# Two weight sums of every third block made by accumulating transfers, weight sums as additions, and a new order inside halved blocks

## The chip, the cores and the metric

The kernel runs on one core of a Trainium2 chip. The metric is device time in microseconds (us) of one execution. Engines are named as in the profile: PE multiplies matrices, DVE (VectorE) and ACT (ScalarE) work on whole tiles of 128 partitions, POOL (GpSimd) issues the transfers that accumulate, SP (SyncE) issues the loads. The kernel has three results before: the median is 1452.87 us (1452.65 to 1453.44).

## The reference

The reference is one decoder layer on a sequence of 256 tokens of width 2048, in float32: a mixing part (block-sparse attention and a gated short convolution, each through its branch weights), then an MLP, then a gated embedding of each layer. Cut to the MLP, which is where the change is:

```
h  = rms_norm(x, g_mlp)
u  = square(relu(h @ w_up))      # 256 x 8192
x  = x + u @ w_down              # 8192 -> 2048
```

The output goes on to the gated embedding and is written out as 256 x 2048.

## The kernel before, in words

**Precision.** Each float32 operand is split into a high part in a faster float32 format and the remainder: ACT copies the tile (`high`), DVE subtracts the copy from the source (`low`). A product is three matmuls, high by high, high by low and low by high. So each weight tile costs an ACT copy and a DVE subtraction ahead of its matmuls.

**The MLP's steps.** The MLP runs as 72 steps, numbered g. Each of the first 64 steps multiplies one 128-column tile of w_up by all of h (`cols`, 32 matmuls into one bank of PSUM, bank 7, called ps_up). ACT copies that bank out (`up`), DVE adds its two halves (`a<-up`), ACT does relu and square, and the result is one 128-row slice of u. The last eight steps take tiles of w_down directly in the same way (ps_dn).

**Blocks.** The rest of w_down is multiplied by the method of seven products in place of eight: a block is a 2 x 2 arrangement of weight pieces B11, B12, B21, B22 (each 128 x 512), and a 2 x 2 of pieces of u. Sums of weight pieces (T1 to T4) and sums of u pieces (S1 to S4) are formed on DVE, and seven products are accumulated in seven banks. There are 56 blocks. Block a = (side, j) is made in one step and multiplied by PE in the next, behind that step's `cols`. Per full block DVE does: `low` of B11 and B22 (`b_lo`, 128x1024), two sums in one instruction of 128x1024 (`raw_s<-raw_s`), a sum of 128x512, `low` of B21 (`b`, 128x512), a sum of 128x512, and `low` of T1/T3 and of T2/T4 (`t_lo`, two of 128x1024). A block whose u sums don't exist yet (called fresh here) adds four sums of 128x128 (`s_raw`) and their `low` (`s`, 128x512). The two tiles of w_up per step add two `w_lo` of 128x1024.

**Halved blocks.** Blocks (0,0), (0,9) and (0,24) to (0,31) are spread over two steps each: the first makes B11, B22 and T1, T3, the second B21 and T2, T4. The last sixteen steps that make blocks, 55 to 70, are all of this kind.

**Parts and jobs.** The seven banks hold one side of the output. When the run of blocks of a side ends, ACT copies the banks out (`part`) and POOL stores them to DRAM, adding to what is there (`part_P`, seven transfers). This comes six times, around steps 10, 18, 27, 35, 43 and 51; four of the stores are carried into the next step. In steps 54 to 66 the finished parts are fetched again (`raw_p`, through the ring of four large tiles that the weights use too), scaled and combined, two small jobs per step. The last job of each is `turn`: DVE transposes in blocks, POOL stores the turned tiles (turned_s), reads them back in the other order (part_in), and adds them to r_kept in DRAM. Toward the end `load_r` loads r from r_kept, and `dn_done` adds the direct results (y_dn) to it, both on POOL. ACT and DVE then make the input of the gated embedding from r (`enter_high`, `enter_low`).

**Order.** The order on PE, DVE, ACT and SP is the order in which the code is written. POOL's DMA issues stand in the order written too. `make` writes the steps of one block; the function passed to it as `evacuate` is the copy `up` (or `dn`) of the step's bank, and PE's next step can start only when that copy is done. `fill` emits a pending part store if there is one. `half_tiles` takes weight tiles from two rings of eight, tags hi and lo; for half of the blocks, T2/T4 used a spare ring of two, tag t.

Of the kernel before, what the change touches and what calls it, by code (L numbers as in the profile page):

```python
# [8 lines left out]
F32 = mybir.dt.float32  # L9
# [29 lines left out]
def hybrid_block_kernel(ctx: ExitStack, tc: tile.TileContext, ins: dict, out: bass.AP):  # L39
# [632 lines left out]
    def half_tiles(name, spare=False):  # L672
        return tuple(wp.tile([P, HALF], F32R, tag="t" if spare else t, name=f"{name}_{t}", bufs=2 if spare else None) for t in ("hi", "lo"))
# [9 lines left out]

    def load_pair(a):

        side, j = a
        q, k, n0 = j // 8, 2 * (j % 8), 8 * side
        raw = wp.tile([P, 4, CW], F32, tag="raw", name="raw_s", bufs=4)
        for i, (n, d) in enumerate(((0, 0), (4, 1), (4, 0), (0, 1))):
            n += 16 * q + n0  # L690
            src = ins["w_down"][n:n + 4, :, (k + d) * P:(k + d + 1) * P]
            load(raw[:, i, :].rearrange("p (n m) -> p n m", n=4), src.rearrange("n p m -> p n m"))
        wS[a] = {"raw": raw}

    def sum_u(j):
# [21 lines left out]
    def make(a, xs, evacuate):  # L717
# [4 lines left out]
        flat = "p a f -> p (a f)"  # L722
        fresh = None
        if 0 in xs:
# [22 lines left out]
        if 0 in xs:  # L747
            dve.tensor_sub(raw[:, 0:3:2, :], raw[:, 0:2, :], raw[:, 2:3, :].to_broadcast([P, 2, CW]))
        if 2 in xs:
            dve.tensor_add(raw[:, 1, :], raw[:, 1, :], raw[:, 0, :])  # L750
            low(b21[1], raw[:, 3, :], b21[0])
            dve.tensor_sub(raw[:, 3, :], raw[:, 1, :], raw[:, 3, :])
        if fresh is not None:
            low(sl, fresh, sh)
        halves = "p (a f) -> p a f"
        if 0 in xs:
            t13 = w["t13"] = half_tiles("t13")
            keep(w, ("T1", "T3"), *t13)
            view = [t.rearrange(halves, a=2) for t in t13]
            high(view[0], raw[:, 0:3:2, :])  # L760
            fill()
            low(view[1], raw[:, 0:3:2, :], view[0])
        if 2 in xs:
            t24 = half_tiles("t24", items.index(a) % 2 == 0)
            keep(w, ("T2", "T4"), *t24)
            view = [t.rearrange(halves, a=2) for t in t24]
            high(view[0], raw[:, 1:4:2, :])
            fill()
            low(view[1], raw[:, 1:4:2, :], view[0])
# [151 lines left out]
    for g in range(NU):  # L921
# [277 lines left out]
```

## Time and profile before

| what | value |
|---|---|
| median of three runs | 1452.87 us |
| profiled execution, its own time | 1451.77 us |
| its span | 1450.0 us |
| busy: PE, DVE, ACT, POOL | 98%, 79%, 61%, 15% |
| steps 8 to 53 of the MLP | 681.69 to 1166.45 us |
| steps 54 to 66 | 1166.45 to 1298.51 us |
| steps 67 to 70 | 1298.51 to 1330.63 us |

Times of the trace are us from the start of the span. The profiled execution took 1.77 us more than its span. A row of a timeline gives the start, the length, the engine, the line of the code (that of the helper which emits it), the operation with the tile written and the tiles read, the shape, how many instructions the row holds, and in brackets how long the engine stood idle before it and what ended that. PE's rows are pipelined: a matmul is longer than the distance to the next.

### The profile page before, as it was taken

How to read it: one execution, taken by the hardware profiler on the slowest of the kernel's cores; microseconds unless marked ns; L12 is line 12 of the kernel's file. 1: busy time of each engine (PE TensorE's matmuls, PEld its weight loads, DVE VectorE, ACT ScalarE, POOL GpSimd, SP SyncE). 2: the span in 40 equal slices, each digit the busy share in tenths (PEclk: the TensorE clock that was granted, in tenths of full speed). 3: DMA queues.
4: the chain of work that ended last, by engine and by line, in shares of the span. 5: the costliest groups of instructions: out<-in, count | busy, mean ns of one | idle time of the engine just before them, and what ended most of it. 6: DMA issues, size and time to landing. Idle time of an engine off the chain costs nothing.

```text
span 1450.0 us, 19774 instructions
## 1 busy us (share of the span) xinstructions
PE 1420.0 (98%) x7009; PEld 1194.6 (82%) x7009; DVE 1144.8 (79%) x1722; ACT 884.8 (61%) x1438; POOL 220.4 (15%) x343
## 2 busy tenths in 40 slices
PE   9999999999999999999999999999999998889998
PEld 7888888888888888888887888888788887778888
DVE  7676566666565657757999999999999998888984
ACT  6765545554544445446777777777777776656652
POOL 0033564402020200000100101001010102242000
PEclk9999999999999999999999999999999999989999
DMA  9867787766665665644765867769686767999370
GB/s 289 295 223 251 230 249 229 234 208 202 209 225 202 215 254 199 222 157 153 221 233 188 264 200 202 244 196 247 202 232 207 206 215 239 279 282 270 135 265 23
DMA packets 208371, 318.81 MB, mean 220 GB/s; under 512 B 13840, under 2 KB 134928, under 8 KB 194192
## 3 DMA queue, kind: packets, MB, share of 16 engines
q1 hardware_dynamic: 190272, 280.79, 59.1%
q0 software_dynamic: 17856, 36.72, 10.3%
q8 instruction: 55, 0.90, 0.2%
q14 instruction: 44, 0.36, 0.1%
q10 hardware_dynamic: 144, 0.04, 0.0%
HBM read 290.23 MB, written 26.74 MB: 219 GB/s over the span
## 4 chain that ended last, share of the span: by engine, by line
PE 58%; DVE 26%; issue 7%; ACT 6%; DMA 2%; POOL 0%; SPq 0%; DVEq 0%; ACTq 0%; POOLq 0%
PE ps_g L90 12%; PE ps_o L90 7%; PE ps_pg L90 6%; PE ps_y L90 6%; DVE w_lo L101 6%; DVE raw_s L101 5%; DVE b_lo L101 4%; DVE t_lo L101 4%; PE ps_up L90 3%; PE ps_q L90 3%; PE ps_k L90 3%; PE ps_cx L90 3%; PE ps_cb L90 3%; PE ps_cc L90 3%; PE ps_v L90 3%
## 5 line engine op out<-in xcount | busy, mean ns | idle before, releaser
L101 DVE TENSOR_TENSOR w_lo<-raw,w_hi 128x512 fp32r<-128x512 f32 (+1 forms) x524 | 467.9, 926 | 186.6 <-ACT w_hi L87 161.5
L87 ACT ACTIVATE w_hi<-raw 128x512 fp32r<-128x512 f32 (+1 forms) x524 | 407.3, 816 | 262.4 <-PE ps_g L90 63.1
L90 PE MATMUL ps_up<-x,w_hi 128*128 128x512 f32 x1024 | 260.1, 397 | 15.1 <-ACT up L87 15.1
L90 PEld LDWEIGHTS ps_up<-x,w_hi 128*128 128x128 f32 x1024 | 192.3, 190 | 63.5 <-ACT up L87 26.4
L87 ACT ACTIVATE t_hi<-raw_s 128x1024 fp32r<-128x1024 f32 x112 | 119.0, 1062 | 126.8 <-DVE raw_s L101 125.4
L90 PE MATMUL ps_g<-w_hi,x 128*128 128x512 f32 x512 | 158.2, 389 | 0.0
L101 DVE TENSOR_TENSOR raw_s<-raw_s 128x1024 f32<-128x1024 f32 x168 | 146.0, 869 | 5.4
L101 DVE TENSOR_TENSOR t_lo<-raw_s,t_hi 128x1024 fp32r<-128x1024 f32 x112 | 134.7, 1220 | 16.7 <-ACT t_hi L87 16.7
L90 PEld LDWEIGHTS ps_up<-x,w_lo 128*128 128x128 f32 x1024 | 131.3, 191 | 5.0
L90 PE MATMUL ps_up<-x,w_lo 128*128 128x256 f32 x1024 | 132.8, 283 | 0.0
L90 PE MATMUL P<-t_hi,s 128*128 128x512 f32 x336 | 121.7, 389 | 0.0
L90 PEld LDWEIGHTS ps_g<-w_hi,x 128*128 128x128 f32 x512 | 96.1, 188 | 20.0
L800 POOL DMA_DIRECT2D part_P<-part x42 | 31.9, 777 | 485.9 <-ACT part L87 404.4
L90 PE MATMUL ps_g<-w_lo,x 128*128 128x512 f32 x256 | 99.6, 389 | 0.0
L90 PE MATMUL ps_y<-w_hi,x 128*128 128x512 f32 x256 | 79.4, 389 | 0.0
L90 PEld LDWEIGHTS P<-t_hi,s 128*128 128x128 f32 x336 | 63.1, 188 | 12.7
L101 DVE TENSOR_TENSOR b_lo<-raw_s,b_hi 128x1024 fp32r<-128x1024 f32 x56 | 68.2, 1218 | 3.6 <-ACT b_hi L87 3.6
L90 PE MATMUL ps_pg<-x,w_hi 128*128 128x512 f32 (+1 forms) x272 | 68.4, 381 | 1.3 <-DVE x L101 1.3
L90 PE MATMUL P<-t_lo,s 128*128 128x512 f32 x168 | 65.4, 389 | 0.0
L87 ACT ACTIVATE a<-a 128x256 f32<-128x256 f32 x128 | 53.2, 415 | 16.9 <-DVE a L101 15.0
L87 ACT ACTIVATE b_hi<-raw_s 128x1024 fp32r<-128x1024 f32 x56 | 58.8, 1050 | 3.2 <-DMA raw_s<-in_w_down_dram 3.2
L90 PEld LDWEIGHTS ps_pg<-x,w_hi 128*128 128x128 f32 x272 | 49.2, 189 | 10.1 <-DVE x L101 2.6
(234 smaller groups left out, 2488.9 us busy)
## 6 DMA issues: line engine op xcount, KB each, us to landing
raw<-in_w_up_dram SPq DMA_DIRECT2D x64, 1024.0 KB, 7.6
raw<-in_w_in_dram SPq DMA_DIRECT2D x56, 1024.0 KB, 5.3
raw_s<-in_w_down_dram SPq DMA_DIRECT2D x224, 256.0 KB, 4.3
raw<-in_w_branch_dram SPq DMA_DIRECT2D x16, 1024.0 KB, 5.7
raw<-in_w_o_dram SPq DMA_DIRECT2D x16, 1024.0 KB, 5.0
raw_first<-in_w_qkv_dram SPq DMA_DIRECT2D x48, 256.0 KB, 6.8
raw<-in_w_qkv_dram SPq DMA_DIRECT2D x12, 1024.0 KB, 6.2
part_P<-part POOLq DMA_DIRECT2D x42, 256.0 KB, 7.3
```

The lines of the kernel that those rows point to most:

```text
L87: return inorder(nc.scalar.activation(*args, **kw))
L90: return inorder(nc.tensor.matmul(*args, **kw))
L101: return lambda *args, **kw: inorder(getattr(nc.vector, name)(*args, **kw))
L800: nc.gpsimd.dma_start(parts[side, name], st, **how)
```

## The change

1. Every third block from the fifth to the forty-seventh (15 blocks) is "added". Its first two weight sums, B11 + B12 and B22 + B12 in the new signs, are no longer made by DVE. SP loads B12 twice into a tile `t13` of the spare ring, two steps ahead, and POOL issues two transfers with `accum_op=add` that bring B11 and B22 onto it. The piece B12 isn't loaded into `raw` for these blocks.
2. All weight sums are additions; the signs move into the u sums and the scalings (`scaled` gets a parameter for subtraction).
3. The copy `up` (`evacuate`) stands right behind the copy of B11 and B22, ahead of the copy of the u sums.
4. T2/T4 always come from the rings hi and lo.
5. In halved blocks DVE has other work between a sum and the `low` that needs ACT's copy of it: the second half makes both sums first, then `low` of B21, then the jobs; the first half runs the jobs between `low` of the u sums and `low` of T1/T3. Since the jobs are now run from inside `make` in these places, a step with a full block runs none.

```diff
-    def half_tiles(name, spare=False):
-        return tuple(wp.tile([P, HALF], F32R, tag="t" if spare else t, name=f"{name}_{t}", bufs=2 if spare else None) for t in ("hi", "lo"))
+    def half_tiles(name):
+        return tuple(wp.tile([P, HALF], F32R, tag=t, name=f"{name}_{t}") for t in ("hi", "lo"))
...
+    ADDED = set(items[4:2 * N_BOTH:3])
...
+    BLOCKS = ((0, 0), (4, 1), (4, 0), (0, 1))
     def load_pair(a):
...
+        for i, block in enumerate(BLOCKS):
+            if i != 2 or a not in ADDED:
+                load(raw[:, i, :].rearrange("p (n m) -> p n m", n=4), pair_part(a, *block))
+
+    def load_added(a):
+
+        wS[a] = {}
+        if a in ADDED:
+            t = wS[a]["t13"] = wp.tile([P, 2, CW], F32, tag="t", name="t13", bufs=2)
+            view = [t[:, i, :].rearrange("p (n m) -> p n m", n=4) for i in range(2)]
+            for i in range(2):
+                load(view[i], pair_part(a, *BLOCKS[2]))
+            for i in range(2):
+                nc.gpsimd.dma_start(view[i], pair_part(a, *BLOCKS[i]), accum_op=ALU.add)
...
             high(hi, src)
-            fill()
+            evacuate()
             if fresh is not None:
                 high(sh, fresh)
-            fill()
             low(lo, src, hi)
-            evacuate()
+            if a in ADDED:
+                t13 = w["t13"]
+            else:
+                t13 = raw[:, 0:3:2, :]
+                dve.tensor_add(t13, raw[:, 0:2, :], raw[:, 2:3, :].to_broadcast([P, 2, CW]))
+            w["raw13"] = t13
         if 2 in xs:
...
-            if 0 not in xs:
-                evacuate()
+            evacuate()
             fill()
+            dve.tensor_add(raw[:, 1, :], raw[:, 1, :], w["raw13"][:, 0, :])
+            if 0 in xs:
+                low(b21[1], raw[:, 3, :], b21[0])
+                dve.tensor_add(raw[:, 3, :], raw[:, 1, :], raw[:, 3, :])
+                raw24 = raw[:, 1:4:2, :]
+            else:
+                dve.tensor_add(raw[:, 2, :], raw[:, 1, :], raw[:, 3, :])
+                low(b21[1], raw[:, 3, :], b21[0])
+                raw24 = raw[:, 1:3, :]
+                work()
         if 0 in xs:
...
+            if fresh is not None:
+                low(sl, fresh, sh)
+            if 2 not in xs:
+                work()
...
+        for a, x in staged[g + 2]:
+            if x == 0:
+                load_added(a)
...
+        def run_jobs():
+            for _ in range(min(2, len(jobs))):
+                jobs.pop(0)()
+
         fill(carried)
         if staged[g]:
-            make(staged[g][0][0], [x for _, x in staged[g]], take)
+            make(staged[g][0][0], [x for _, x in staged[g]], take, run_jobs)
         take()
-        for _ in range(min(2, len(jobs))):
-            jobs.pop(0)()
```

On DVE, the work of one added block that is not fresh (made in step 10), first before the change, then after it. `t_6098` is the tile t13 that the transfers fill; `raw_s` is the block's loaded tile.

```order
L101 TENSOR_TENSOR x<-a,x 128x256
L101 TENSOR_TENSOR b_lo<-raw_s,b_hi 128x1024
L101 TENSOR_TENSOR raw_s<-raw_s 128x2x512
L101 TENSOR_TENSOR raw_s<-raw_s 128x512
L101 TENSOR_TENSOR b_1_6386<-raw_s,b_0_6385 128x512
L101 TENSOR_TENSOR raw_s<-raw_s 128x512
L101 TENSOR_TENSOR t_lo<-raw_s,t_hi 128x1024 x2
L101 TENSOR_TENSOR a<-up 128x256
```

```order
L101 TENSOR_TENSOR x<-a,x 128x256
L101 TENSOR_TENSOR b_lo<-raw_s,b_hi 128x1024
L101 TENSOR_TENSOR raw_s<-raw_s,t_6098 128x512
L101 TENSOR_TENSOR b_1_6390<-raw_s,b_0_6389 128x512
L101 TENSOR_TENSOR raw_s<-raw_s 128x512
L101 TENSOR_TENSOR t_lo<-t_6098,t_hi 128x1024
L101 TENSOR_TENSOR t_lo<-raw_s,t_hi 128x1024
L101 TENSOR_TENSOR a<-up 128x256
```

The 128x2x512 sum (shown as 128x1024 in the profile) is gone, and the first 128x512 sum and the first `t_lo` read the tile t13.

On DVE, the second half of block (0,24) (step 56), first before, then after. `raw_p` are the fetched parts; `blocks` are their transposes.

```order
L101 TENSOR_TENSOR raw_s<-raw_s 128x512
L101 TENSOR_TENSOR b_1_11136<-raw_s,b_0_11135 128x512
L101 TENSOR_TENSOR raw_s<-raw_s 128x512
L101 TENSOR_TENSOR t_lo<-raw_s,t_hi 128x1024
L101 SCALAR_TENSOR_TENSOR raw_p<-raw_p,scales 128x256 x2
L101 STREAM_TRANSPOSE blocks<-raw_p 128x512 x2
L101 TENSOR_TENSOR a<-up 128x256
```

```order
L101 TENSOR_TENSOR raw_s<-raw_s 128x512 x2
L101 TENSOR_TENSOR b_1_11177<-raw_s,b_0_11176 128x512
L101 SCALAR_TENSOR_TENSOR raw_p<-raw_p,scales 128x256 x4
L101 TENSOR_TENSOR t_lo<-raw_s,t_hi 128x1024
L101 TENSOR_TENSOR a<-up 128x256
```

The jobs moved ahead of `t_lo`, and they are other jobs: the transposes that stood in step 56 stand in step 57 after the change, as each later pair of jobs stands one step later.

## Rows read from the trace of the kernel before

**Rows 1.** The page's busy line, and DVE's busy share in 40 equal slices of the span, in tenths.

```profile
PE 1420.0 (98%) x7009; PEld 1194.6 (82%) x7009; DVE 1144.8 (79%) x1722; ACT 884.8 (61%) x1438; POOL 220.4 (15%) x343
...
DVE  7676566666565657757999999999999998888984
```

**Rows 2.** Busy time by stretch: length, then PE, PEld, DVE, ACT and POOL busy (instructions), PE's granted clock, the DMA engines' share and GB/s. Steps 8 to 53, 54 to 66 and 67 to 70.

```profile
681.69:1166.45 484.76, 476.89 (x2419) 402.01 (x2418) 466.66 (x610) 357.26 (x520) 31.89 (x42) 1.00 0.73 219
1166.45:1298.51 132.06, 117.93 (x576) 98.33 (x575) 119.42 (x178) 80.63 (x118) 34.61 (x52) 0.94 0.81 247
1298.51:1330.63 32.12, 32.09 (x172) 27.49 (x171) 28.62 (x41) 18.05 (x22) 11.42 (x16) 1.00 1.01 287
```

**Rows 3.** The same view for steps 14 to 21, one by one: a dense step, a step with fresh sums, the step of the part stores, and the sum of the eight.

```profile
745.20:755.53 10.33, 10.33 (x55) 8.86 (x53) 10.19 (x16) 7.58 (x11) 0.00 (x0) 1.00 0.69 220
...
766.29:777.48 11.19, 10.64 (x53) 8.78 (x54) 11.05 (x17) 7.87 (x12) 0.00 (x0) 1.00 0.60 197
...
799.00:809.76 10.76, 10.49 (x54) 8.68 (x52) 8.82 (x11) 9.23 (x16) 3.78 (x7) 1.00 0.95 295
...
sum 85.35, PE 83.81 PEld 70.59 DVE 82.52 ACT 62.67 POOL 3.78; mean PE 10.48 PEld 8.82 DVE 10.31 ACT 7.83 POOL 0.47
```

**Rows 4.** Waits from 681 to 1166 us: who waited for whom, in total, times, and the longest, in us.

```profile
ACT t_hi L87 <- DVE raw_s L101: 92.8, 90, 2.0
PE ps_up L90 <- ACT up L87: 7.9, 21, 0.6
```

**Rows 5.** ACT's timeline in step 49, a fresh one.

```profile
1122.28 0.63 ACT L87 ACTIVATE s<-s_raw 128x512 fp32r<-128x512 f32 x1 [1.26 <-DVE s_raw L101]
1122.82 0.58 ACT L87 ACTIVATE up<-ps_up 128x512 f32<-128x512 f32 x1
```

**Rows 6.** PE's timeline at the start of step 50.

```profile
1123.45 0.96 PE L90 MATMUL ps_up<-x,w_hi 128*128 128x512 f32 x3 [0.55 <-ACT up L87]
```

**Rows 7.** Groups of DVE instructions of one shape from 640 to 1400 us: busy us, mean ns of one, idle time before them.

```profile
L101 DVE TENSOR_TENSOR raw_s<-raw_s 128x1024 f32<-128x1024 f32 x56 | 68.6, 1225 | 1.9
```

**Rows 8.** DVE's timeline in steps 54 to 66.

```profile
1181.76 1.00 DVE L101 SCALAR_TENSOR_TENSOR raw_p<-raw_p,scales 128x256 f32<-128x256 f32 x2
1182.68 0.42 DVE L101 TENSOR_TENSOR a<-up 128x256 f32<-128x256 f32 x1
...
1207.33 1.23 DVE L101 TENSOR_TENSOR raw_s<-raw_s 128x1024 f32<-128x1024 f32 x1
1208.47 0.68 DVE L101 TENSOR_TENSOR s<-s_raw,s 128x512 fp32r<-128x512 f32 x1
1209.67 1.22 DVE L101 TENSOR_TENSOR t_lo<-raw_s,t_hi 128x1024 fp32r<-128x1024 f32 x1 [0.52 <-ACT t_hi L87]
...
1218.19 1.23 DVE L101 TENSOR_TENSOR t_lo<-raw_s,t_hi 128x1024 fp32r<-128x1024 f32 x1 [1.13 <-ACT t_hi L87]
...
1293.23 2.31 DVE L101 TENSOR_TENSOR w_lo<-raw,w_hi 128x1024 fp32r<-128x1024 f32 x2
...
1299.46 1.23 DVE L101 TENSOR_TENSOR t_lo<-raw_s,t_hi 128x1024 fp32r<-128x1024 f32 x1 [1.19 <-ACT t_hi L87]
1300.60 2.35 DVE L101 TENSOR_TENSOR w_lo<-raw,w_hi 128x1024 fp32r<-128x1024 f32 x2
```

**Rows 9.** ACT's timeline, two waits for loads in steps 63 and 65.

```profile
1258.08 2.01 ACT L87 ACTIVATE w_hi<-raw 128x1024 fp32r<-128x1024 f32 x2 [1.92 <-DMA raw<-in_w_down_dram]
...
1284.42 1.06 ACT L87 ACTIVATE b_hi<-raw_s 128x1024 fp32r<-128x1024 f32 x1 [2.06 <-DMA raw_s<-in_w_down_dram]
```

**Rows 10.** PE's timeline, the starts of steps 58 and 66.

```profile
1207.36 1.11 PE L90 MATMUL ps_up<-x,w_hi 128*128 128x512 f32 x3 [3.30 <-ACT up L87]
...
1287.71 2.50 PE L90 MATMUL ps_dn<-x,w_hi 128*128 128x512 f32 x5 [3.82 <-ACT dn L87]
```

**Rows 11.** The chain behind the last turn: POOL's timeline (its first and its last transfer), the landing of the last one (KB each, us from issue to landing), and ACT's first read of what it brings.

```profile
1293.01 2.16 POOL L826 DMA_DIRECT2D turned_s<-blocks  x4 [6.24 <-DVE blocks L101]
...
1328.92 0.89 POOL L903 DMA_DIRECT2D r<-y_dn  x1 [0.42 <-DVE y_dn L101]
...
r<-y_dn POOLq DMA_DIRECT2D x1, 128.0 KB, 6.6
...
1338.01 0.91 ACT L87 ACTIVATE x<-r,vec 128x256 fp32r<-128x256 f32 x2
```

**Rows 12.** The DMA view of two windows of 20 us: from 976 to 996 the queue of POOL's transfers (packets, MB, share of 16 engines) and the landing of its part stores (KB each, median us), and from 1000 to 1020 the queue of SP's loads.

```profile
q0 software_dynamic: 1008, 1.84, 56.0%
...
part_P<-part POOLq DMA_DIRECT2D x6, 256.0 KB, 8.7
...
q1 hardware_dynamic: 4565, 4.53, 68.5%
```

**Rows 13.** A window with part stores, 885 to 916: its busy time as in rows 2, the landing of the raw_s loads issued from 896 to 911, and ACT's copy of the piece B21 of one of these blocks.

```profile
885.00:916.00 31.00, 30.75 (x158) 26.04 (x157) 28.85 (x34) 24.07 (x37) 6.10 (x7) 1.00 1.01 262
...
DMA to landing us min/median/max: 6.3/6.9/12.6
...
909.17 0.62 ACT L87 ACTIVATE b<-raw_s 128x512 fp32r<-128x512 f32 x1
```

**Rows 14.** DVE's and POOL's timelines at a set of part stores, step 52.

```profile
1152.14 1.23 DVE L101 TENSOR_TENSOR w_lo<-raw,w_hi 128x1024 fp32r<-128x1024 f32 x1 [0.17 <-ACT w_hi L87]
...
1152.89 1.75 POOL L800 DMA_DIRECT2D part_P<-part  x2 [0.57 <-ACT a L87]
```

More of the change, by code (lines that the diff above doesn't have):

```diff
@@ L682, in unit_half, with pair_part @@
         return lambda: high(hi, raw), lambda: low(lo, raw, hi)
+    ADDED = set(items[4:2 * N_BOTH:3])
+    def pair_part(a, n, d):
+        side, j = a
+        n += 16 * (j // 8) + 8 * side
+        k = 2 * (j % 8) + d
+        return ins["w_down"][n:n + 4, :, k * P:(k + 1) * P].rearrange("n p m -> p n m")
+    BLOCKS = ((0, 0), (4, 1), (4, 0), (0, 1))
     def load_pair(a):
-        side, j = a
-        q, k, n0 = j // 8, 2 * (j % 8), 8 * side
         raw = wp.tile([P, 4, CW], F32, tag="raw", name="raw_s", bufs=4)
[L689 to L693, printed above, removed]
+        wS[a]["raw"] = raw
+        for i, block in enumerate(BLOCKS):
[10 more added lines that the diff above has]
+                nc.gpsimd.dma_start(view[i], pair_part(a, *BLOCKS[i]), accum_op=ALU.add)
     def sum_u(j):
@@ L743, in make @@
             high(b21[0], raw[:, 3, :])
-            if 0 not in xs:
-                evacuate()
+            evacuate()
             fill()
-        if 0 in xs:
[L748 to L757, printed above, removed]
+            dve.tensor_add(raw[:, 1, :], raw[:, 1, :], w["raw13"][:, 0, :])
[8 more added lines that the diff above has]
+                work()
+        if 0 in xs:
+            if fresh is not None:
+                low(sl, fresh, sh)
+            if 2 not in xs:
+                work()
+            t13 = half_tiles("t13")
             keep(w, ("T1", "T3"), *t13)
             view = [t.rearrange(halves, a=2) for t in t13]
-            high(view[0], raw[:, 0:3:2, :])
+            high(view[0], w["raw13"])
             fill()
-            low(view[1], raw[:, 0:3:2, :], view[0])
+            low(view[1], w["raw13"], view[0])
         if 2 in xs:
-            t24 = half_tiles("t24", items.index(a) % 2 == 0)
+            t24 = half_tiles("t24")
             keep(w, ("T2", "T4"), *t24)
             view = [t.rearrange(halves, a=2) for t in t24]
-            high(view[0], raw[:, 1:4:2, :])
+            high(view[0], raw24)
             fill()
-            low(view[1], raw[:, 1:4:2, :], view[0])
+            low(view[1], raw24, view[0])
     PRODUCTS = ((("P1", "A11", "B11", 0, 3), ("P3", "S4", "B22", 0, 3)),
@@ L800, in store, with scaled @@
         nc.gpsimd.dma_start(parts[side, name], st, **how)
-    def scaled(dst, src, by, plus):
-        dve.scalar_tensor_tensor(dst, src, by, plus, op0=ALU.mult, op1=ALU.add)
+    def scaled(dst, src, by, other, how=ALU.add):
+        dve.scalar_tensor_tensor(dst, src, by, other, op0=ALU.mult, op1=how)
     ORDER = ("P5", "P4", "P2", "P3", "P1", "P7", "P6")
@@ L1058, in hybrid_block_kernel @@
     enter_low(15)
-    scaled(c12, prod["P6"], up0, e)
-    scaled(c22, prod["P5"], down1, u3)
+    scaled(c12, prod["P6"], down0, e)
+    scaled(c22, prod["P5"], up1, u3, ALU.subtract)
     half_gate(0, 1)
```

18 lines of the change are left out of this document (9 added, 9 removed).

## The prediction

> **What bounds the kernel now.** I read the page's busy shares and slices first, then busy time by stretch, then single steps, then the waits, and last the timelines of DVE, ACT and POOL where the change touches them.
>
> PE is busy 98% of the span, which looks like the end of the matter, but a PE that waits for a bank still counts as busy here. DVE stands at nine tenths or more in a row only from slice 20 to slice 33 (689 to 1196 us) [rows 1]; that is the MLP. Four stretches matter [rows 2]: steps 8 to 53 (484.76 us), steps 54 to 66 (132.06 us), steps 67 to 70, and the tail. In the first DVE is busy 466.66 us of 484.76, in the second 119.42 of 132.06, while PE's clock there falls to 0.94 because PE waits.
>
> A step in which PE is never late takes 10.33 us (the first row of [rows 3]). Eight steps, one whole round of the block pattern, take 85.35; eight times 10.33 is 82.64. So 2.71 us per eight steps is PE's wait on something else, and DVE is that: the steps of four fresh sums (11.19 us) have DVE busy 11.05, and only the step of the seven part stores (799.00) leaves it about 2 us idle [rows 3]. The waits say the same: ACT's largest is for DVE's weight sums (92.8 us), and PE waits in its turn for ACT's copy out of the bank, `up` [rows 4]. In fresh steps that copy stands behind the copy of `s`, which waits 1.26 us for DVE, and PE then starts 0.55 us late [rows 5, 6]. Over 46 steps, two of them short, the excess is 44 / 8 x 2.71, about 14.9 us. That is the most the full stretch can give.
>
> **Part by part.** *Two sums by transfers.* 15 of the 46 steps lose the 128x1024 sum. One takes 1225 ns [rows 7]; its slot, from its start to the next start, is 1208.47 - 1207.33 = 1.14 us [rows 8]. DVE saves 15 x 1.14 = 17.1 us, per eight steps 17.1 x 8 / 46 = 3.0, so it needs 85.35 - 3.0 = 82.4 where PE needs 82.64. DVE goes just below PE, PE becomes the bound, and most of the 14.9 comes back: I take 13.5, bounds 9 and 14.9. The low bound is for pockets where fresh steps with one added block among four still cost DVE more than 10.33; the earlier copy of `up` (next) is what evens these out.
>
> *`up` ahead of `s`.* In the fresh steps the bank comes free 1.26 + 0.54 = 1.8 us sooner [rows 5]. In the dense steps that is hidden already. It is no term of its own: it lets DVE's surplus in one step be repaid in the next without PE seeing it. Bounds 0 and the 0.55 us of [rows 6] in about 20 fresh steps, 11 us, which lies inside the 14.9.
>
> *Halved blocks.* Before, DVE stands 0.52 us (steps of b and s) and 1.13 us (steps of b21) ahead of `t_lo`, waiting for ACT's `t_hi` [rows 8]. After, the jobs stand in these gaps, and they are long enough (0.87 to 1.8 us). The jobs of step 54 are no longer run there, because a full block doesn't call them: the whole chain of jobs is one step later, and so is the last turn, in step 66 in place of 65. DVE starts step 55 at 1182.68 [rows 8]; after, 17.1 us plus the 1.00 of step 54's jobs earlier, near 1164.6. From there to the end of the last turn, where w_lo starts, it took 1293.23 - 1182.68 = 110.5 us. Take away the gaps, 6 x 0.52 + 5 x 1.13 = 8.8. Add what stands ahead of the turn in step 66: from 1293.23 to 1300.60 less the wait of 1.19 and the slot of t_lo, 1300.60 - 1299.46, that is 5.0, and the 1.00 of the job that left step 54. That gives 1272.3. Now the loads: raw_p's buffers come free a step later and the loads behind them land later. Before, ACT already waited 1.92 and 2.06 us for such loads [rows 9]. I add 8 us over the 12 steps, four waits of the size of [rows 9]; bounds 0 (those two as they are, which the 110.5 holds already) and 18 (one of 2 us in nine of the steps). The last turn ends near 1280.3, 12.9 earlier than in the profile.
>
> PE's own gaps here, 3.30 and 3.82 us the largest [rows 10], close by themselves when DVE is early. By PE alone the kernel would end some 25 us sooner: 13.5, these two (7.1), and about 5 of the other waits of the stretch, which are shorter.
>
> *The chain behind the last turn.* This is what turns 25 into less. After the last turn POOL stores the turned tiles, reads them back as part_in, adds them to r_kept, loads r, and adds y_dn: from 1293.2 (the end of the transposes) to 1328.92 + 6.6 = 1335.5 [rows 11], 42.3 us. Four transfers stand in it one behind the other, and each waits for the one before. ACT reads the result at 1338.01 [rows 11], so before it had 2.5 us to spare and decided nothing. After, it starts at 1280.3 and lands at 1322.6, and ACT can read no sooner: 1322.6 - 1338.0 = -15.4. PE would have been there at about -25. The chain therefore sets the end.
>
> *Transfers.* What the DVE doesn't add, the DMA engines do. An added block has one more plain 256 KB load and two accumulating ones of 256 KB in 512 B pieces. The trace has plain ones of that shape: a window with 4.53 MB of loads is 68.5% of 20 us [rows 12], so 256 KB take about 0.8 us of all 16 engines. It has accumulating ones only in longer pieces: 1008 packets, 1.84 MB, 56.0% of 20 us [rows 12], 1.6 us for 256 KB. By bytes the two new ones cost 3.2 us; by packets (178 ns each, 512 of them over 16 engines) 5.7 each, 11.4. I take 2 us each, near the byte end, because a plain transfer of 512 B pieces costs little over its share by bytes. Per three steps (31 us) that is 0.8 + 4 = 4.8, so the share rises from 0.73 [rows 2] to 0.88: still room. Where the part stores run it is 1.01 already [rows 13], raw_s lands 12.6 us after its issue there, and yet ACT's copy of it at 909.17 had no wait [rows 13]. Six such windows, each with one or two added blocks: I put a third to half a microsecond on each, 2 us in all, bounds 0 and 12.
>
> By the Trainium skill (DMA: Bandwidth & Descriptors, "Anatomy of one DMA", the GpSimd path) one such transfer takes 2.0 us plus its bytes over 436e3, that is 2.6 us for 256 KB. The trace disagrees: the part stores land 8.7 us after issue [rows 12], on engines that are busy with other queues. By the rule the 2 us would vanish and the time would be 2 lower.
>
> *POOL* gets 30 issues of 0.86 us [rows 14] where it was idle, in the queue of the part stores. An accumulate waits for its load, and stores behind it wait too; nothing reads those soon. *The signs* cost nothing: same operations, same shapes. *Tiles:* t24 now takes from the ring of 8 each time, five tiles per step in place of 4.5. A tile comes round after 1.6 steps, by when its matmuls are over; if that cover fails it is at most 1 us in a full step.
>
> Sum: -15.4 (chain) + 2 = -13.4 against the profiled run of 1451.8. That run lies 1.1 below the median of the three, 1452.9, so I predict 1452.9 - 13.4 = 1439.5.
>
> **Rivals.** *The chain doesn't bind* (0.13). With PE waiting less in the tail's loads, or fewer late loads than my 8 us, the end follows PE: -20 to -25, near 1430. For it: 42.3 us is latency under a busy DMA (1.01 in the stretch from 1298 [rows 2]), and would shrink if the loads finish early. Against: the same loads are still to be made then.
>
> *Transfers eat it* (0.20). In the windows at share 1.01 t13 isn't there in time: load 12.6 us and accumulation up to 9 or more behind each other, against two steps, 20.7, plus the part of a step until it is read. Each of some ten blocks loses 0.7 us more: -13.4 + 7 = -6, 1447. Against: rows 13 show a margin.
>
> *Slower: DMA becomes the bound* (0.07). If a 512 B accumulating packet costs 178 ns like a 2 KB one, three steps need 0.73 x 31 + 0.8 + 11.4 = 34.8 us of 31: 46 steps take 46 / 3 x 34.8 = 534 in place of 484.8, about 1490 with what is saved later. It decides from 119 ns per packet, where the share reaches 1. For it: no such packet is in the trace. Against: 512 B plain ones are cheap.
>
> *POOL's issues hold DVE* (0.02). If each of 30 issues stopped a DVE operation for its 0.86 us, 26 us would come back: -13.4 + 26 = +13, 1465. Against: the w_lo at 1152.14 took 1.23 us with POOL issuing part stores under it [rows 14], no more than any other. The Trainium skill (SBUF — State Buffer, "Who interferes with whom") says that a VectorE instruction with two SBUF inputs contends with a GpSimd instruction that reads SBUF; w_lo has two such inputs, and this row shows no stop beside DMA issues.
>
> *No change* (0.06): accumulation so late that DVE waits as long as the sum took.
>
> The forecast itself has 0.52.
>
> **How the numbers follow.** A measurement tells 0.2%, 2.9 us, from no change. Faster: 0.52 + 0.13 + 0.20 = 0.85. Same: 0.06. Slower: 0.07 + 0.02 = 0.09. The range reaches from 1430 (the chain doesn't bind) to 1449 (transfers eat most of it); the likeliest case alone spans 1435 to 1444.
>
> **What would show it.** Right: steps 14 to 21 take 82.6 to 83.5 us; 41 sums of 128x1024 instead of 56 in the MLP; no DVE wait ahead of `t_lo` in halved steps; POOL's last r<-y_dn released by r_kept and ACT's read of x<-r waiting for it; a DMA share near 0.88 in the first stretch. Wrong: DVE's first sum waiting for a DMA into t; a DMA share of 1 throughout; raw_s late in many full steps; PE never waiting at the tail.

## The result and the profile after

| | before | after |
|---|---|---|
| median, us | 1452.76 (1452.32 to 1453.44, 4 runs) | 1440.38 (1437.59 to 1441.77, 4 runs) |
| ratio to before | | 0.9912, 95% interval 0.9895 to 0.9929 |
| profiled execution, us | 1451.77 | 1440.91 |
| its span, us | 1450.0 | 1439.1 |
| steps 8 to 53 | 484.76 | 474.78 |
| steps 54 to 66 | 132.06 | 121.75 |
| steps 67 to 70 | 32.12 | 34.14 |
| from step 71 to the end | 119.37 | 126.88 |

The forecast was 1439.5. The kernel is 12.4 us faster by the medians and 10.9 by the two profiled executions. The table shows the shape of it: about 20 us are gained up to step 66 and 9.5 are given back behind it.

Busy time by stretch after the change, columns as in [rows 2]; the second stretch is steps 54 to 66:

```profile
681.55:1156.33 474.78, 471.96 (x2418) 402.87 (x2416) 449.22 (x596) 355.68 (x520) 71.44 (x72) 1.00 0.90 248
1156.33:1278.08 121.75, 112.21 (x574) 94.55 (x575) 113.51 (x169) 80.99 (x118) 29.25 (x44) 0.99 0.84 249
1278.08:1312.22 34.14, 32.17 (x171) 27.40 (x170) 30.93 (x46) 18.07 (x22) 12.43 (x18) 1.00 1.00 299
1312.22:1439.10 126.88, 114.10 (x659) 99.28 (x657) 96.32 (x167) 64.59 (x111) 6.09 (x7) 0.97 0.45 153
```

DVE has 17.4 us less to do in steps 8 to 53 and PE is busy for nearly all of them; the DMA share has gone from 0.73 to 0.90. The same view for steps 14, 16 and 19, and the sum of the eight, beside [rows 3]:

```profile
743.77:754.10 10.33, 10.33 (x55) 8.86 (x53) 10.19 (x16) 7.03 (x11) 0.00 (x0) 1.00 0.84 265
...
764.42:774.75 10.33, 10.33 (x54) 8.86 (x53) 10.21 (x16) 7.82 (x12) 0.00 (x0) 1.00 0.52 172
...
795.40:805.84 10.44, 10.44 (x55) 8.68 (x53) 8.50 (x11) 9.24 (x16) 3.62 (x7) 1.00 0.98 325
...
sum 82.87, PE 82.87 PEld 70.81 DVE 80.10 ACT 62.07 POOL 11.70; mean PE 10.36 PEld 8.85 DVE 10.01 ACT 7.76 POOL 1.46
```

The eight steps took 85.35 us and take 82.87, against 82.64 for a PE that never waits. PE's waits for `up`, 7.9 us in 21 places before [rows 4], are one of 0.8 us (the row of the same view after):

```profile
PE ps_up L90 <- ACT up L87: 0.8, 1, 0.8
```

In the halved blocks the gaps of [rows 8] are closed. DVE's waits for `t_hi` ahead of `t_lo` are 1.0 us in two places from 1156 to 1300, both behind step 66, where they were 10.0 us in 12 from 1166 to 1300. DVE's timeline in steps 55 and 56, after; these `t_lo` have no wait:

```profile
1178.06 1.00 DVE L101 SCALAR_TENSOR_TENSOR raw_p<-raw_p,scales 128x256 f32<-128x256 f32 x2
1178.98 1.22 DVE L101 TENSOR_TENSOR t_lo<-raw_s,t_hi 128x1024 fp32r<-128x1024 f32 x1
...
1184.99 1.79 DVE L101 SCALAR_TENSOR_TENSOR raw_p<-raw_p,scales 128x256 f32<-128x256 f32 x4
1186.70 1.22 DVE L101 TENSOR_TENSOR t_lo<-raw_s,t_hi 128x1024 fp32r<-128x1024 f32 x1
```

The chain behind the last turn, beside [rows 11]: POOL's first transfer of it, its last, and ACT's reads of r for n = 10 and n = 11.

```profile
1282.81 2.20 POOL L852 DMA_DIRECT2D turned_s<-blocks  x4 [0.22 <-issue]
...
1322.35 0.96 POOL L929 DMA_DIRECT2D r<-y_dn  x1
...
1322.26 0.50 ACT L87 ACTIVATE x<-r,vec 128x256 fp32r<-128x256 f32 x1
1327.70 0.51 ACT L87 ACTIVATE x<-r,vec 128x256 fp32r<-128x256 f32 x1 [4.95 <-DMA r<-y_dn]
```

Before, ACT read both at once, at 1338.01, and waited for nothing. Now the read of n = 11 waits 4.95 us for the last transfer of the chain, and all that follows waits with it. That is where the time from step 71 on goes; why steps 67 to 70 take 2.0 us more no run singles out. The steps themselves were ready sooner. ACT's copy of the last direct result, before and after:

```profile
1336.37 0.60 ACT L87 ACTIVATE dn<-ps_dn 128x512 f32<-128x512 f32 x1 [0.57 <-PE ps_dn L90]
```

```profile
1319.32 0.57 ACT L87 ACTIVATE dn<-ps_dn 128x512 f32<-128x512 f32 x1
```

That is 17.05 us earlier, and the read that waits for the chain is 10.7 us earlier.

### The profile page after: what moved, and what is told of

The parts are those of the page before. It is cut to its first block, busy times and chain, and to the rows that moved or that the text cites. A ratio compares the mean times of both kernels' runs of the same rounds, so it can differ in the third digit from the quotient of the medians.

```text
span 1439.1 us, 19915 instructions
## 1 busy us (share of the span) xinstructions
PE 1410.3 (98%) x7009; PEld 1191.7 (83%) x7009; DVE 1127.1 (78%) x1707; ACT 883.8 (61%) x1438; POOL 259.5 (18%) x373
## 4 chain that ended last, share of the span: by engine, by line
PE 69%; DVE 12%; DMA 11%; issue 4%; ACT 2%; POOL 1%; SPq 0%; DVEq 0%; POOLq 0%; ACTq 0%
PE ps_g L90 12%; PE ps_up L90 11%; PE P L90 7%; PE ps_o L90 7%; PE ps_pg L90 6%; PE ps_y L90 6%; PE ps_k L90 3%; PE ps_q L90 3%; PE ps_v L90 3%; PE ps_cx L90 3%; PE ps_cb L90 3%; PE ps_cc L90 3%; DMA part_in<-turned_s 3%; DVE w_lo L101 2%; DVE t_lo L101 2%
## 5 line engine op out<-in xcount | busy, mean ns | idle before, releaser
L90 PE MATMUL ps_up<-x,w_hi 128*128 128x512 f32 x1024 | 254.3, 391 | 6.3 <-ACT up L87 6.3
L87 ACT ACTIVATE t_hi<-raw_s 128x1024 fp32r<-128x1024 f32 x97 | 103.0, 1062 | 115.5 <-DVE raw_s L101 115.5
L101 DVE TENSOR_TENSOR raw_s<-raw_s 128x512 f32<-128x512 f32 (+1 forms) x138 | 117.3, 850 | 5.4 <-DMA raw_s<-in_w_down_dram 1.1
L101 DVE TENSOR_TENSOR t_lo<-raw_s,t_hi 128x1024 fp32r<-128x1024 f32 x97 | 116.9, 1219 | 4.4 <-ACT t_hi L87 4.4
L711 POOL DMA_DIRECT2D t<-in_w_down_dram x30 | 39.1, 1556 | 320.1 <-DVE raw_s L101 94.0
L101 DVE TENSOR_TENSOR b_lo<-raw_s,b_hi 128x1024 fp32r<-128x1024 f32 x56 | 68.3, 1220 | 3.8 <-ACT b_hi L87 3.8
```

The costliest lines, as they stand in the source:

```text
L87: return inorder(nc.scalar.activation(*args, **kw))
L90: return inorder(nc.tensor.matmul(*args, **kw))
L101: return lambda *args, **kw: inorder(getattr(nc.vector, name)(*args, **kw))
L711: nc.gpsimd.dma_start(view[i], pair_part(a, *BLOCKS[i]), accum_op=ALU.add)
```

## The experiments

The edits are to the changed kernel. Each was timed against the kernel before; the ratio and its interval stand with each median.

**No added block (e1).**

```diff
-    ADDED = set(items[4:2 * N_BOTH:3])
+    ADDED = set()
```

> The changed kernel with no added block: DVE makes all sums again, everything else of the change stays. Theory (the added blocks take DVE off the bound in steps 8 to 53, and the rest gives nothing by itself): eight steps take 85 us again, steps 8 to 53 about 484 us, DMA share there back to 0.73, the last turn ends 10 us later and so does the kernel: 1450 us. Rival (the gain is that of the new order in halved blocks and of the earlier copy of up): 1443 us or less, with the last turn within 3 us of where it is.

Measured: 1453.23 us, 1.0004 (0.9995 to 1.0013). Without the added blocks the whole gain is gone; the copy order and the order in halved blocks by themselves gain no time. Steps 8 to 53 and steps 54 to 66, then steps 18 and 19, a fresh one and the one of the part stores:

```profile
681.79:1165.91 484.12, 477.07 (x2418) 401.30 (x2417) 466.65 (x610) 357.13 (x520) 31.66 (x42) 1.00 0.73 219
1165.91:1290.44 124.53, 113.18 (x576) 95.67 (x574) 115.32 (x173) 80.62 (x117) 30.82 (x47) 0.97 0.81 246
...
786.71:797.88 11.17, 10.63 (x54) 8.79 (x54) 11.07 (x16) 7.92 (x12) 0.00 (x0) 1.00 0.60 188
797.88:809.80 11.92, 11.12 (x53) 8.54 (x53) 9.95 (x12) 10.17 (x18) 3.78 (x7) 1.00 0.96 287
```

The earlier copy let PE run ahead for a few steps, and the loss came back where DVE caught up with it: step 19 took 10.76 before [rows 3] and takes 11.92 here. A bound that is moved in time is still the bound.

The time hides a gain. Steps 54 to 66 took 132.06 us before and take 124.53 here, so the new order does gain 7.5 us there. The chain takes it back: the last turn stands in step 66, its transposes start at 1292.73 (1292.01 before), and ACT reads r for n = 11 when it did before, at about 1338.4, after a wait:

```profile
1338.25 0.51 ACT L87 ACTIVATE x<-r,vec 128x256 fp32r<-128x256 f32 x1 [4.29 <-DMA r<-y_dn]
```

So the added blocks gain their time in steps 8 to 53, and by that they also start the chain sooner, which lets the other gain show.

**The copy of `up` put back (e5).**

```diff
             high(hi, src)
-            evacuate()
             if fresh is not None:
                 high(sh, fresh)
             low(lo, src, hi)
+            evacuate()
```

> The changed kernel with the copy of up put back behind the copy of s in fresh blocks. Theory (it is no term of its own, it only evens out steps in which DVE is late): PE waits for up in some of the 20 fresh steps, 0 to 0.5 us each, the time 1440 to 1444 us. Rival (the earlier copy is what lets PE keep 10.33 us in fresh steps): more than 0.3 us lost in each fresh step and 1446 us or more.

Measured: 1440.80 us, 0.9914 (0.9898 to 0.9929), no different from the changed kernel. PE waits for `up` 1.4 us in two places of steps 8 to 53, against 0.8 in one. With the added blocks DVE is early enough; the copy's place is worth nothing that these runs can tell.

**The old order in halved blocks (e2).**

```diff
             else:
-                dve.tensor_add(raw[:, 2, :], raw[:, 1, :], raw[:, 3, :])
                 low(b21[1], raw[:, 3, :], b21[0])
+                dve.tensor_add(raw[:, 2, :], raw[:, 1, :], raw[:, 3, :])
                 raw24 = raw[:, 1:3, :]
-                work()
...
-            if 2 not in xs:
-                work()
...
         take()
+        run_jobs()
```

> The changed kernel with the old order in halved blocks: jobs behind t_lo, run in full blocks too, low of B21 between the two sums. Theory (the order fills DVE's gaps, some 9 us, but puts the last turn a step later and raw_p's buffers free later, and the chain behind the last turn sets the end): DVE waits 0.52 and 1.13 us ahead of t_lo again, the last turn stands in step 65 and ends within 3 us of 1283, and the time is 1440 us, give or take 3. Rival (the new order in halved blocks is worth what it takes out of DVE's waits): 1448 us or more.

Measured: 1440.63 us, 0.9912 (0.9899 to 0.9925): the same time as the changed kernel, by another way. The edit does two things: it restores the old order, and it runs the jobs in step 54 again. Steps 54 to 66 take 129.05 us here, 7.3 more than after, and the tail 122.56, 4.3 less:

```profile
1153.32:1282.37 129.05, 113.34 (x576) 94.02 (x575) 113.54 (x171) 80.76 (x118) 31.58 (x47) 0.99 0.83 248
1282.37:1316.74 34.37, 32.93 (x171) 27.25 (x170) 30.76 (x44) 17.95 (x22) 12.95 (x19) 1.00 1.01 295
1316.74:1439.30 122.56, 114.46 (x658) 100.23 (x658) 96.35 (x167) 64.37 (x111) 3.12 (x3) 0.96 0.45 151
```

The last turn stands in step 65 again, its transposes at 1281.38, and ACT's read of r (n = 10, 11) at 1326.21 waits for no transfer. So here the steps set the end (from 1270 to the read the chain of waits runs over DVE and ACT, `w_lo`, `raw_s` and `t_hi`), and after the change the transfers do. The two come out equal by accident, and part of that is that steps 8 to 53 took 3.5 us less in this execution (471.26), though their code is the same from step 26 on.

**y_dn of n = 10 and 11 off the chain (e3).**

```diff
-        if n < 12:
+        if n < 10:
             nc.gpsimd.dma_start(to, y, accum_op=ALU.add)
```

> The changed kernel with y_dn of n = 10 and 11 added to r by DVE in place of a transfer from POOL's queue, so that ACT's reads of r for n = 10 and 11 don't stand behind the chain that follows the last turn. Theory (that chain sets the end): ACT's read of n = 11 comes near 1322.5 in place of 1327.7, and the time is 1435 us; DVE pays 0.42 us twice. Rival (PE, or the late loads, set the end and the chain is only beside it): no change, 1440 us.

Measured: 1436.83 us, 0.9879 (0.9862 to 0.9896), 3.6 us under the changed kernel where 5 was expected; the two intervals only touch. ACT reads both at 1324.41 with no wait, later than the 1322.5 expected: ahead of it the copies of P (`p`) start 1.83 us late, and the chain of waits puts r_kept<-part_in ahead of them.

**Two raw_p in the ring t (e9).**

```diff
-        t = wp.tile([P, 8, S], F32, tag="raw", name="raw_p", bufs=4)
+        if h == 0:
+            t, rest = (wp.tile([P, 4, S], F32, tag="t", name="raw_p", bufs=2) for _ in range(2))
+        else:
+            t = wp.tile([P, 8, S], F32, tag="raw", name="raw_p", bufs=4)
+            rest = t[:, 4:8, :]
```

> The changed kernel with two of the four raw_p fetches (the first and the third) in the two tiles of the ring t, which has no user after step 53, in place of the weights' ring of four. Theory (the halved steps lose time because raw_p holds the weights' ring a step longer and the loads behind it come late): ACT's and DVE's waits for loads in steps 54 to 70 fall from 15.5 us to 8 or less, the last turn ends 5 to 7 us sooner, and with it the chain and the kernel: 1434 us. Rival (the loads are late because the DMA engines are full there, 0.84, whatever ring they use): waits as before and 1440 us.

Measured: 1436.36 us, 0.9882 (0.9869 to 0.9895), 4.0 us under the changed kernel where 6 was expected. In the changed kernel ACT and DVE wait 15.5 us for loads from 1156 to 1280:

```profile
ACT w_hi L87 <- DMA raw<-in_w_up_dram: 7.6, 4, 3.1
...
ACT w_hi L87 <- DMA raw<-in_w_down_dram: 4.3, 3, 2.7
ACT b_hi L87 <- DMA raw_s<-in_w_down_dram: 2.5, 2, 1.7
DVE raw_s L101 <- DMA raw_s<-in_w_down_dram: 1.1, 1, 1.1
```

Here, in the same window, 1.8 us:

```profile
ACT w_hi L87 <- DMA raw<-in_w_down_dram: 1.1, 1, 1.1
ACT b_hi L87 <- DMA raw_s<-in_w_down_dram: 0.7, 1, 0.7
```

The ring was the cause and not the DMA engines, whose share here is no lower than after (0.86 and 0.84 up to the last turn's transposes). From the start of step 54 to these transposes it is 120.0 us (1277.88 - 1157.92), 5.5 less than after (1281.80 - 1156.33 = 125.5). The end moves with the chain, for which ACT still waits:

```profile
1323.88 0.51 ACT L87 ACTIVATE x<-r,vec 128x256 fp32r<-128x256 f32 x1 [6.20 <-DMA r<-y_dn]
```

**The transfers without their gain (e6).** The tile t13 is loaded and added to, and nothing reads it.

```diff
-            t = wS[a]["t13"] = wp.tile([P, 2, CW], F32, tag="t", name="t13", bufs=2)
+            t = wS[a]["unread"] = wp.tile([P, 2, CW], F32, tag="t", name="t13", bufs=2)
...
-            if i != 2 or a not in ADDED:
+            if True:
...
-            if a in ADDED:
-                t13 = w["t13"]
-            else:
-                t13 = raw[:, 0:3:2, :]
-                dve.tensor_add(t13, raw[:, 0:2, :], raw[:, 2:3, :].to_broadcast([P, 2, CW]))
+            t13 = raw[:, 0:3:2, :]
+            dve.tensor_add(t13, raw[:, 0:2, :], raw[:, 2:3, :].to_broadcast([P, 2, CW]))
```

> The changed kernel in which the 15 added blocks still load B12 twice and add to it by the two transfers, but nothing reads that tile: DVE makes the sums as before (so these blocks load B12 a third time). It has the transfers' cost without their gain. Theory (512 B accumulating pieces cost about 2 us of all engines per 256 KB, and the queue has room for them): against e1_no_added, 1453.2 us, no more than 2 us, so 1453 to 1455 us, with a DMA share near 0.9 in steps 8 to 53. Rival (the transfers cost time by themselves, which the DVE's saving has paid for): 1458 us or more.

Measured: 1455.21 us, 1.0017 (1.0008 to 1.0025), 2.0 us over the kernel with no added block; the intervals still overlap. Steps 8 to 53 take 486.55 us, 2.4 more than there, at a share of 0.90. The transfers' own cost is small at that load, while DVE is the bound.

**Every second block added (e7).**

```diff
-    ADDED = set(items[4:2 * N_BOTH:3])
+    ADDED = set(items[4:2 * N_BOTH:2])
```

> The changed kernel with every second block added (22 in place of 15). DVE saves 7 x 1.14 = 8 us more. Theory (PE is the bound in steps 8 to 53 already, so more relief gives nothing there but the 2 to 4 us of its waits in steps 44 and 53): seven times (0.8 + 2 x 2.04) of DMA time bring the share from 0.90 to 0.97, and the time is 1438 to 1442 us. Rival 1 (DVE still bounds): 1433 us or less. Rival 2 (the transfers are at their limit): loads and t tiles come late in most steps, 1447 us or more.

Measured: 1442.65 us, 0.9931 (0.9918 to 0.9944), a little outside the first range and not told apart from the changed kernel by the intervals. DVE does 7.7 us less, the stretch takes the same time at a share of 0.98, and DVE's waits for part_P grow to 9.8 us:

```profile
681.58:1156.76 475.18, 472.45 (x2419) 404.93 (x2418) 441.55 (x589) 355.84 (x521) 90.44 (x86) 1.00 0.98 260
...
DVE b L101 <- DMA part_P<-part: 9.8, 3, 5.3
```

Over half of that wait (5.27 us) stands ahead of step 53, which takes 14.96 us; no other step of the stretch takes more than 10.5. So PE bounds the stretch with 15 added blocks already. The part stores land 12.3 us after their issue here (median; 7.8 after).

**Two added blocks moved (e10).** The full stretch gained 10.0 us where I had put 13.5. Two places hold the difference: step 44 and its successor (11.55 and 10.47 us in place of 10.33 each) and step 53 (12.95). What stands ahead of them on ACT, DVE and POOL, after:

```profile
998.82 1.06 ACT L87 ACTIVATE t_hi<-t 128x1024 fp32r<-128x1024 f32 x1 [3.71 <-DMA t<-in_w_down_dram]
...
1149.24 0.69 DVE L101 TENSOR_TENSOR b<-raw_s,b 128x512 fp32r<-128x512 f32 x1 [4.05 <-DMA part_P<-part]
...
1135.63 2.60 POOL L711 DMA_DIRECT2D t<-in_w_down_dram  x2 [3.00 <-DMA t<-in_w_down_dram]
1137.13 5.54 POOL L826 DMA_DIRECT2D part_P<-part  x5
```

The first row is the tile of item 31, issued in the step of the part stores and late by 3.71 us. The others are a queue: POOL waits 3.00 us for the load under item 46's accumulation, the part stores go out behind it, and DVE, which needs one of the 44 slots for `low` of B21, waits until a store has landed.

```diff
-    ADDED = set(items[4:2 * N_BOTH:3])
+    ADDED = {items[i - (i in (31, 46))] for i in range(4, 2 * N_BOTH, 3)}
```

> The changed kernel with two of its 15 added blocks moved one place ahead: items 30 and 45 in place of 31 and 46, so that no accumulating transfer is issued in the step in which POOL stores parts, with all else the same. Theory (the full stretch loses 4 us of the 13.5 that I expected to these two: item 31's tile is late and puts DVE behind until step 44, item 46's accumulation stands ahead of five part stores, whose slots DVE then waits for in step 53): no wait of DVE for part_P and none of ACT for t, steps 44 and 53 near 10.4 us, step 54 starts near 1153, the time 1437 us. Rival (the late transfers are those of a full DMA, and fall on other blocks then): waits as before, 1440 us.

Measured: 1438.08 us, 0.9901 (0.9888 to 0.9915). The time doesn't tell it from the changed kernel. The stretch is 3.4 us shorter at the same share of 0.90:

```profile
682.68:1154.10 471.42, 471.30 (x2418) 403.40 (x2417) 450.10 (x596) 356.45 (x520) 71.41 (x72) 1.00 0.90 250
```

ACT no longer waits for t. The wait for a slot is not gone: DVE has one of 2.34 us for part_P at 988.72, where it has slack to cover it.

One pair of executions is not enough here, since the losses come and go. The starts of the steps in PE's timeline of the other kernels settle one of the two places. With item 46 in place step 53 takes 12.95 us after, and 10.33, 12.20, 11.46 and 14.06 in e2, e3, e5 and e9. With item 46 moved or left out (e10, c2, c4, c5, c6) it takes 10.33 to 10.47. So the queue in front of the stores is what step 53 loses to, in four executions of five. Step 44 takes 10.33 to 12.00 in the first group and 10.33 to 11.04 in the kernels with both blocks moved: that item 31 costs it anything is not shown, though the late t is there in each kernel of the first group and in none with both moved. The stretch is 471.3 to 475.1 us in the first group and 470.8 to 471.8 with both moved.

**Everything that helped, and more jobs (c2).** Four edits at once: those of e3 and e9, item 46 left out, and this one.

```diff
-    ADDED = set(items[4:2 * N_BOTH:3])
+    ADDED = set(items[4:2 * N_BOTH - 3:3])
...
             make(staged[g][0][0], [x for _, x in staged[g]], take, run_jobs)
+            if len(staged[g]) == 2:
+                run_jobs()
```

> e3's and e9's edits together, the jobs run in step 54 too, so that the last turn stands in step 65 again, and the last added block (item 46) left to DVE. Theory: the chain behind the last turn starts 13 us earlier and no longer sets the end, PE does: 1429 us, with ACT's copies of P and its reads of r ahead of the last gate waiting for no transfer. Rival (the tail is set by PE and DVE already once y_dn is off the chain): no better than e3, 1436 us.

Measured: 1444.78 us, 0.9937 (0.9922 to 0.9951), 4.4 us over the changed kernel by the medians (the intervals overlap a little) and well over e3 and e9, whose edits it has; 1429 was expected. The last edit is not what the expectation says: a full block has four pieces in that list and a halved one two, so it ran two further jobs in each halved step and none in step 54. The last turn came at 1247.91, 34 us early, and the chain was far off the end. Yet DVE waited 10.74 us for a slot that part_in held until its transfer had landed, and ACT 3.51 us for raw_p, whose jobs now came ahead of the data:

```profile
1267.33 0.69 DVE L101 TENSOR_TENSOR s<-s_raw,s 128x512 fp32r<-128x512 f32 x1 [10.74 <-DMA r_kept<-part_in]
...
1217.51 1.05 ACT L87 ACTIVATE raw_p<-raw_p,scales 128x256 f32<-128x256 f32 x2 [3.51 <-DMA raw_p<-part_P]
```

**The same jobs, with part_in off the slots (c5).** The edits of e10 and e3, the two further jobs per halved step (its expectation speaks of step 54 too), and

```diff
-                st = slot([P, 2, S], F32, "part_in")
+                st = wp.tile([P, 4, S], F32, tag="t", name="part_in", bufs=2)[:, 0:2, :]
```

> e10's blocks, e3's y_dn on DVE, and c2_all's jobs in step 54, but with part_in in the two tiles of ring t in place of slots, and raw_p all in the weights' ring. Theory (in c2_all the u sum waited 10.7 us for a slot that part_in held until its transfer had landed): that wait is gone and so are ACT's waits for slots at the tail; the loads stay late as in the changed kernel: 1433 to 1436 us. Rival (the earlier jobs themselves crowd the halved steps): 1440 us or more with no wait for part_in's transfer.

Measured: 1439.48 us, 0.9911 (0.9897 to 0.9924). The wait for part_in's slot is gone, as the theory has it, but the gain to 1436 or less is not there: ACT waits 15.3 us for raw_p in three places. This is the rival's outcome in mechanism. Four jobs a step ask for the parts before they are in.

```profile
ACT raw_p L87 <- DMA raw_p<-part_P: 15.3, 3, 7.6
```

**The three gains together (c4).** The edits of e3, e9 and e10, with the jobs as in the changed kernel.

> e10's blocks, e3's y_dn on DVE and e9's raw_p in the ring t together, without the jobs in step 54 of c2_all. Theory (the three act on different waits, and c2_all was slow only because its jobs stand a step earlier and the slots of part_in run out): the three gains of 3.5, 4 and 4 us add up for the most part: 1430 to 1432 us. Rival (y_dn on DVE or raw_p in t is what held c2_all up): 1438 us or more, with a wait of DVE for r_kept<-part_in.

Measured: 1428.16 us, 0.9829 (0.9815 to 0.9842), the fastest of all, 12.2 us under the changed kernel, below the range expected. The three alone promised 9.9 (3.6 + 4.0 + 2.3); the 2.3 more is within what these medians can be off (the four runs of e3 alone span 6.3). Both stretches are shorter than after:

```profile
681.68:1153.34 471.66, 471.11 (x2419) 403.44 (x2417) 450.22 (x597) 356.06 (x521) 71.15 (x72) 1.00 0.90 250
1153.34:1268.92 115.58, 111.50 (x576) 94.37 (x574) 112.21 (x168) 80.61 (x117) 29.14 (x44) 0.99 0.88 264
```

**What the order in halved blocks is worth there (c6).** The last kernel with the old order, the jobs kept in their steps.

```diff
             else:
-                dve.tensor_add(raw[:, 2, :], raw[:, 1, :], raw[:, 3, :])
                 low(b21[1], raw[:, 3, :], b21[0])
+                dve.tensor_add(raw[:, 2, :], raw[:, 1, :], raw[:, 3, :])
...
         take()
+        if len(staged[g]) == 2:
+            run_jobs()
```

> c4_tail_moved with the old order inside halved blocks (low of B21 between the sums, jobs behind t_lo), the jobs staying in the steps where the changed kernel has them, so that the last turn is in step 66 as before. It asks what the order by itself is worth where the chain behind the last turn no longer hides it. Theory (it fills DVE's gaps of 0.52 and 1.13 us): DVE waits for t_hi again in all twelve steps, the last turn ends 6 to 9 us later, and the time is 1434 to 1437 us against 1428.2. Rival (PE and the loads bound the halved steps, the gaps are free): 1428 to 1430 us.

Measured: 1437.19 us, 0.9890 (0.9873 to 0.9907), 9.0 us over the kernel with the new order. The last turn's transposes start at 1284.11 in place of 1272.61. DVE's waits ahead of `t_lo` from 1150 to 1345, here and then in the kernel with the new order:

```profile
DVE t_lo L101 <- ACT t_hi L87: 13.2, 16, 1.1
```

```profile
DVE t_lo L101 <- ACT t_hi L87: 2.1, 4, 0.5
```

The new order is thus worth about as much time as its gaps hold (11.1 us of waits, 9.0 of time), once neither late loads nor the chain take it away again. This edit was not run on the changed kernel: e2 also puts the jobs back into step 54, and it is the two together that are worth nothing there.

## Why the prediction was right

Its steps in turn:

- **DVE bounds the full stretch, the added blocks relieve it.** Right, and shown by taking them away: the stretch is 484.12 again. The 128x1024 sums are 41, at 1225 ns as before:

```profile
L101 DVE TENSOR_TENSOR raw_s<-raw_s 128x1024 f32<-128x1024 f32 x41 | 50.2, 1225 | 2.4 <-DMA raw_s<-in_w_down_dram 1.1
```

  Eight steps came to 82.87, inside the 82.6 to 83.5.
- **13.5 us in that stretch.** Mis-sized: 10.0. The step that failed is the one on transfers beside part stores. I had put 2 us in all on six windows; in this execution it cost 1.36 us in steps 44 and 45 and 2.62 in step 53, 4.0 together, and nothing in most of the others. I had the late tile as a rival; it came true in one block (item 31). The slots I had not seen at all: I wrote that nothing reads the part stores soon, which is true, but DVE waits for the room that they occupy. The whole is no fixed cost: the same steps lost nothing in e2.
- **`up` ahead of `s` is no term of its own.** Right (1440.80 without it).
- **Gaps in halved blocks closed, loads late by 8 us.** The gaps are closed, and the loads are late: ACT and DVE wait 15.5 us for them where the kernel before waited 6.8, 8.7 more. But the 8 us stood on DVE's path, and there they cost about 4.1: from DVE's start of step 55 to the end of the last turn it is 111.8 us, and 107.7 by the forecast's own sum without loads (110.5 - 8.8 + 5.0 + 1.0). That the jobs stand a step later is not all of the cause either: in e2, with the jobs in step 54 again, these waits are 10.5 us (1153 to 1300). The rows of before, from 1166 to 1300:

```profile
ACT b_hi L87 <- DMA raw_s<-in_w_down_dram: 3.2, 2, 2.1
ACT w_hi L87 <- DMA raw<-in_w_down_dram: 2.7, 2, 1.9
ACT w_hi L87 <- DMA raw<-in_w_up_dram: 0.9, 2, 0.8
```

- **The last turn at 1280.3.** It ended at 1283.0, 2.7 later, and that is two errors that partly cancel. DVE came to step 55 at 1171.19 (the row that stood at 1182.68 in [rows 8]), 6.6 us after the 1164.6 forecast:

```profile
1171.19 0.42 DVE L101 TENSOR_TENSOR a<-up 128x256 f32<-128x256 f32 x1
```

  The forecast had moved DVE by its whole saving of 17.1 us, while the stretch, which PE bounds then, got 10.0 shorter. From there the late loads cost 3.9 less than forecast.
- **By PE alone the end would come 25 us sooner.** Wrong: ACT's copy of the last direct result came 17.05 us sooner (1336.37 and 1319.32). PE's gaps did not close by themselves. From 1166 to 1300 PE waited 14.2 us for ACT before, and from 1156 to 1300 after it waits 12.4. The late loads stand behind most of that: up to 1280 it is 10.5 us, and 3.7 in e9, where the loads are in time. The chain hid this error. By this row the kernel without the chain would have ended near 1436 (1452.9 - 17, an estimate) and not near 1430; e3 came out at 1436.83.
- **The chain sets the end.** Right: e3 takes the last transfer off the path and gains 3.6 us, e9 starts the chain 3.9 earlier and gains 4.0. Its length was mis-sized a little: from 1283.0 to ACT's read at 1327.70 it is 44.7 us, not 42.3. The read came 10.7 us earlier than the second one of the row at 1338.01 in [rows 11] (1338.4), not 15.4.
- **The sum.** Against the profiled run I had -13.4 and it was -10.9, 2.5 less. The late turn and the longer chain, 2.7 and 2.4, less the 2 us that I had added for transfers, make 3.1 of it; the rest is mostly the 0.4 us between the two reads of the row at 1338.01. The medians moved by 12.4, since the profiled run of before was 1.0 under its median and that of after 0.5 over. So the mechanism was right, and the close agreement with 1439.5 is luck for a good part.
- **Transfers at 2 us each.** Right. The queue of POOL's transfers over steps 8 to 53, before and after:

```profile
q0 software_dynamic: 5152, 11.01, 11.2%
```

```profile
q0 software_dynamic: 20978, 18.85, 24.3%
...
t<-in_w_down_dram POOLq DMA_DIRECT2D x30, 256.0 KB, 7.4
```

  Before, 42 part stores take 0.112 x 484.76 = 54.3 us of all engines, 1.29 each. After, the queue takes 0.243 x 474.78 = 115.4; if the stores cost what they did, that leaves 61.1 for 30, an estimate of 2.04 us each. In e7 the same sum gives 2.0 for each of 44 (0.299 x 475.18 less 54.3). The slower rival, 5.7 us each, is out. The median landing is 7.4 us at a share of 0.90. By the fit in the Trainium skill (DMA: Bandwidth & Descriptors, "Anatomy of one DMA") the estimate is 2.6 us; this trace doesn't agree, and the measured landing decides.
- **POOL's issues hold no DVE operation.** Right. An accumulating issue is longer than I took, 39.1 us for 30, 1.3 each, but `t_lo` took 1219 ns in the mean with 1220 before. The Trainium skill (SBUF — State Buffer, "Who interferes with whom") says that a VectorE instruction with two SBUF inputs contends with a GpSimd instruction that reads SBUF; beside these issues no such cost shows.

What stays open: why step 71 to the end is still 4 us longer in the fastest kernel (1426.3 - 1302.86 = 123.4, against 119.37 before). Up to ACT's reads of r for n = 10 and 11 (at 1312.76) it is 9.9 us against 7.38, and 1.6 more lie behind them; no run takes either apart. That c2_all lost its time to slots and early jobs is read from its waits; each cause alone was not run.

## What to carry to other kernels

Before you relieve a bound engine, look for the chain of transfers that runs beside it to the same end, and take its slack (here 2.5 us) as the most that the rest can gain over the chain's own earlier start before the chain decides. An accumulating transfer needs more than DMA time: it stands in a queue in front of stores, and whoever shares their buffers can wait too (step 53), so don't issue it in the steps in which that queue is already used. And an edit that measures as nothing can have its gain hidden behind the next wait: the new order took 7.5 us out of steps 54 to 66 in e1 and none off the time, and it is worth 9.0 between c6 and c4. Read the stretches and not only the end, and try such an edit again after each bound that falls.

## What the runs showed of the hardware

The accumulating 256 KB transfer into SBUF cost an estimated 2.04 us of all 16 engines in pieces of 512 B, against 1.29 us for the part stores to DRAM in longer ones: some four times the pieces, 1.6 times the cost. The two also differ in direction, and not every store accumulates, so the piece length alone is not shown to be the cause.

A tile whose store stands in POOL's queue stays occupied until the store has landed: DVE waited 4.05 us for one after the change and 10.74 us in c2. The part stores landed 7.8 us after issue (median) at a share of 0.90 and 12.3 at 0.98 (e7), where 14 more accumulating transfers pass through the same queue.
